# Other places for the background steps of the conv-GeGLU layers, in a two-network fp32 kernel

## The chip, the cores and the metric

One program on one core of a Trainium2 chip. The metric is the device time of one execution in microseconds, the median of several runs. The kernel before takes 2448.88 us (three runs: 2448.77, 2448.88, 2451.74).

Engines in the text: PE (TensorE, matrix products), DVE (VectorE), ACT (ScalarE), POOL (GpSimd) and SP (SyncE, which issues most DMAs). PSUM is the memory of eight banks into which PE writes.

## The reference

Two small networks run one behind the other on a sequence of 512 positions with 1024 channels, in fp32. The first has a pooling mixer, a conv-GeGLU layer (ffn0), windowed attention and a second conv-GeGLU layer (ffn1). The second has an S5 mixer, an MLP, an SSD mixer and an MLP; its norms are shifted and scaled by a vector `mod` worked out from a conditioning vector `c`.

```
def conv_glu_ffn(h, w_in, conv_w, conv_b, w_out):
    u = h @ w_in                                   # 1024 -> 2 * 2816
    up = jnp.pad(u, ((0, 0), (CONV_WIDTH - 1, 0), (0, 0)))
    u = sum(conv_w[k] * up[:, k:k + S] for k in range(CONV_WIDTH)) + conv_b
    gate, val = jnp.split(u, 2, axis=-1)
    return (jax.nn.gelu(gate, approximate=True) * val) @ w_out
...
x = x + rms_norm(conv_glu_ffn(rms_norm(x, ffn_pre_g), ...), ffn_post_g)
...
mod = silu(c) @ ada_w[i] + ada_b[i]                # 1024 -> 6144, for the second network
```

## The kernel before

Activations are held transposed: 128 channels on the partitions, 512 positions along the row. Each fp32 operand is split into a high and a low part, and each product is three matmuls (L220 to L222: hi·hi, lo·hi, hi·lo). A weight chunk comes by a DMA into `ws` (three buffers), ACT copies the high part `wh` (L205) and DVE subtracts for the low part `wl` (L206).

**A conv-GeGLU layer** (`ffn_layer`) has 22 column tiles of the hidden width, in three phases (8, 8 and 6 tiles). A phase handles its tiles two by two. For one pair PE fills four PSUM banks (`pp`: gate and value of two tiles); `scaled` (L969, DVE) multiplies each bank by the norm's factor into `u` and so frees it; `glu` does the convolution (ACT, then DVE L975 and L976), gelu on ACT, the product (L983) and the split into `hi` (ACT L319) and `lo` (DVE L321). The pool for these products has four banks, so the matmuls of one pair need those of the one before read. After phases 0 and 1 `project` multiplies by the part of `w_out` for the tiles so far, in eight output tiles, and `evac` copies (phase 0, ACT L1007) or adds (phase 1, DVE L1009) each into `f`. The last phase's products are done by the tail (`tail_`), first for the first 256 positions and then for the second 256, and the next layer's norm (`acc`, L305 sums over channels, L311 and L314 the factor) and its first projection are joined to it: the first half of the next layer's head needs only the first half of the tail. `seam` (L815) orders this.

**Background work** is done by generators that a layer steps on through `bg[0](n)`: each generator in the list is taken n steps further (class `Background`). In ffn0 it is `s5_tables` (tables for the S5 mixer, many 128x512 and 128x128 operations on DVE, L681 to L793; 72 steps), and what has not been done by the end of the layer's body is drained there (`end_tables`). In ffn1 it is `vecmat` (L477), which works out `mod` (12 blocks) and a like product with S5's input weights (2 blocks), 60 steps in all, and in addition Toeplitz matrices for S5. A block of `vecmat` takes eight tiles `as` of 128x512 (256 KB each, two buffers, DMA issued by POOL, L495). DVE multiplies the first by its factor (L498) and multiplies and adds the next seven into `aa` (L500); after every second tile the generator yields, so a step is two tiles. At a block's end ACT casts `aa` into bf16 three times (L512), DVE taking off each time what has been cast (L514), and PE sums over the partitions with twelve matmuls (L484, four for each part), which `mod` is built from. Since `aa` has one buffer, the next block's L498 follows the casts.

A layer's Python code gives only priorities: the scheduler of the framework orders each engine's instructions ahead of time, with the program's order as priority and a model of durations. Each engine then works through its instructions in that fixed order.

In the layer's body (L1013 to L1046) steps stand in three places: two at the beginning (L1015), `rate` behind each pair (L1039), and one behind each of the eight evacuations of a down phase (L1043). Phase 0 has three pairs in the body (the first belongs to the head), phase 1 four and the last three. `rate` is 5 in ffn0, 4 in ffn1.

Of the kernel before, what the change touches and what calls it, by code (L numbers as in the profile page):

```python
# [62 lines left out]
def net_kernel(ctx: ExitStack, tc: tile.TileContext, I: dict, out: bass.AP, parts=ALL):  # L63
# [27 lines left out]
    def psmm():  # L91
        return psm.tile([P, 512], F32, tag="mm", name=nm("mm"))
# [741 lines left out]
    bg = [no_bg]  # L834
# [125 lines left out]
    def ffn_layer(l, phases, late=None, rate=3):  # L960
# [52 lines left out]
        def body_():  # L1013
            hh, hl = S_["pre"].hi, S_["pre"].lo
            bg[0](2)  # L1015
            for ph, (j0, j1) in enumerate(phases):
                final = ph == len(phases) - 1
                if final and late is not None:
                    late()
                for j in range(j0 if ph else 2, j1, 2):  # L1020
                    pp = {(i, q): psmm() for i in range(2) for q in range(2)}
                    src = [chunks(win, 0, KD, i * F1 + j * P) for i in range(2)]
                    if final and j == j1 - 2:
                        chs = [list(c) for c in src]
                        for q in range(2):
                            for i in range(2):
                                for ch in chs[i]:
                                    mm_chunk(pp[i, q], ch, q, hh, hl, KD, FULL)
                        for i in range(len(tl.runs)):
                            tl.load_apart(i)  # L1030
                    else:
                        for _ in range(2):
                            for i in range(2):
                                ch = next(src[i])
                                for q in range(2):
                                    mm_chunk(pp[i, q], ch, q, hh, hl, KD, FULL)
                    for q in range(2):
                        glu(j + q, *(scaled(pp[i, q]) for i in range(2)))
                    bg[0](rate)  # L1039
                if not final:  # L1040
                    def evac(n, ps, span):
                        down(n, ps, span, ph == 0, False)
                        bg[0](1)  # L1043

                    project(wout, j0, j1 - j0, 0, (0, 8), S_["ah"], S_["al"], evac)
                    S_["ah"], S_["al"] = [], []  # L1046
# [914 lines left out]
    def end_tables():  # L1961
        work.drain()
        close("stk", "psb")
        bgps[0] = psmm
# [5 lines left out]
    for name in names:  # L1970
# [6 lines left out]
        if name == "ffn0":  # L1977
            layer = ffn_layer(0, ((0, 8), (8, 16), (16, 22)),
                              lambda: rope_c.update(rope_tables()) if "attn" in names else None, 5)
            seam(prev, layer)  # L1980
            close("plf")
            if tables_due and "pool" not in names:
                start_tables()
            layer.body()
            if tables_due:
                end_tables()
                tables_due = False
        elif name == "attn":
            layer = attention_layer(opened("atc"), opened("atps", space=PSUM), rope_c or rope_tables())
            seam(prev, layer)  # L1990
            layer.body()
            close("atc", "atps")
        elif name == "ffn1":
            layer = ffn_layer(1, ((0, 8), (8, 16), (16, 22)), rate=4)
            seam(prev, layer)
            if tables_due:
                start_tables()
                end_tables()
                tables_due = False
            if ada_due[:1] == [0]:  # L2000
                start_ada(ada_due.pop(0))
            if toeplitz_due:
                work.gens.append(s5_toeplitz(opened("stz"), dr))
                toeplitz_due = False
            layer.body()
            work.drain()
            close("stz", "adp")
        else:
            if tables_due:
                start_tables()  # L2010
                end_tables()
                tables_due = False
            if toeplitz_due:
                work.gens.append(s5_toeplitz(opened("stz"), dr))
                toeplitz_due = False
            if ada_due and (name[-1] == "1" or name == "ssd" or ada_due[0] == 0):
                start_ada(ada_due.pop(0))
                work.drain()
                close("stz", "adp")
            if name == "s5":  # L2020
                layer = s5_layer(dr, opened("s5p"), opened("s5ps", space=PSUM))
            elif name == "ssd":
                layer = ssd_layer(opened("sdp"), dpl, opened("sdps", space=PSUM))
            else:
                layer = mlp_layer(int(name[-1]))
            seam(prev, layer)
            if name == "mlp0" and ada_due:
                start_ada(ada_due.pop(0))
            layer.body()
            work.drain()  # L2030
            close("adp", "s5p", "s5ps", "sdp", "sdps")
# [41 lines left out]
```

## Time and profile before

| | |
|---|---|
| median of three runs | 2448.88 us |
| profiled execution | 2448.6 us |
| its span | 2446.9 us |
| mean PE clock granted | 0.974 of full |
| PE busy | 2303.6 us |
| DVE busy | 1707.1 us |
| ACT busy | 1139.7 us |
| ffn0's end (last up matmul to attention's first projection) | 417.4 to 481.20 |
| ffn1's end (the same, to S5's first projection) | 1036.6 to 1087.75 |

The profiled execution is 1.7 us longer than its span and 0.3 us shorter than the median. Times in the rows below are microseconds from the span's start. In brackets behind an instruction stands how long its engine had been idle, and what ended the wait.

### The profile page before, as it was taken

The page shows a single profiled execution, that of the slowest core. Times are in us where ns is not written, and L with a number is a line of the kernel's source. Part 1 is how long each engine was busy: PE and PEld are TensorE (multiplying, and loading weights), DVE is VectorE, ACT ScalarE, POOL GpSimd, SP SyncE. Part 2 cuts the span into 40 slices and gives each one's busy share as a digit, 9 for nine tenths or more (in the row PEclk, how much of TensorE's full clock was granted, in tenths as well). Part 3 has the DMA queues.
Part 4 walks back from the last instruction along what each step waited for, and adds up shares of the span by engine and source line. Part 5 has one row for each costly group of instructions (what it writes and reads, how often), then busy time and mean ns, then how long its engine had stood idle before and what let it go on. Part 6 is the DMA issues. An engine that isn't in the chain of part 4 may idle for free.

```text
span 2446.9 us, 33813 instructions
## 1 busy us (share of the span) xinstructions
PE 2303.6 (94%) x12477; PEld 1948.5 (80%) x12477; DVE 1707.1 (70%) x3064; ACT 1139.7 (47%) x2030; POOL 419.4 (17%) x596
## 2 busy tenths in 40 slices
PE   6989998788989999988799999999999999999998
PEld 6778877775878888787779878789878878888888
DVE  6896979767778697886646666666777788533333
ACT  6533535466675343455534333344555554422322
POOL 2001120002431211110301011010242340200110
PEclk9999999889989999989899999999999999999999
DMA  4224453311465655455742555542333332233322
GB/s 123 81 91 137 145 152 118 106 59 45 127 193 174 195 179 190 159 198 170 220 141 73 172 164 189 186 151 74 113 95 99 108 101 89 91 95 98 100 82 74
DMA packets 265190, 315.52 MB, mean 129 GB/s; under 512 B 34161, under 2 KB 222401, under 8 KB 264001
## 3 DMA queue, kind: packets, MB, share of 16 engines
q1 hardware_dynamic: 220929, 233.64, 30.5%
q0 software_dynamic: 19648, 62.41, 8.1%
q10 hardware_dynamic: 24448, 17.31, 2.2%
q8 instruction: 98, 1.61, 0.3%
q14 instruction: 67, 0.55, 0.1%
HBM read 289.12 MB, written 24.18 MB: 128 GB/s over the span
## 4 chain that ended last, share of the span: by engine, by line
PE 63%; DVE 14%; DMA 10%; issue 7%; ACT 4%; POOL 1%; SPq 0%; ACTq 0%; DVEq 0%; POOLq 0%
PE mm L221 18%; PE mm L220 18%; PE mm L222 18%; DMA as<-in_ada_w 6%; DVE wl L206 3%; DVE aa L500 1%; ACT wh L205 1%; PE pb L1746 1%; PE mm L1676 1%; PE mm L1677 1%; PE mm L1678 1%; DMA tz<-d_k 1%; DVE u L969 1%; PE py L1417 1%; DVE aa L514 1%
## 5 line engine op out<-in xcount | busy, mean ns | idle before, releaser
L220 PE MATMUL mm<-h,wh 128*128 128x512 f32 (+1 forms) x1792 | 665.6, 373 | 31.9 <-ACT h L429 16.2
L221 PE MATMUL mm<-h,wh 128*128 128x512 f32 (+1 forms) x1792 | 666.7, 373 | 7.4 <-DVE h L430 3.7
L222 PE MATMUL mm<-h,wl 128*128 128x512 f32 (+1 forms) x1792 | 663.4, 371 | 0.2 <-DVE wl L206 0.2
L205 ACT ACTIVATE wh<-ws 128x1024 fp32r<-128x1024 f32 (+1 forms) x367 | 387.1, 1059 | 505.6 <-PE mm L221 427.6
L206 DVE TENSOR_TENSOR wl<-ws,wh 128x1024 fp32r<-128x1024 f32 (+1 forms) x367 | 462.3, 1262 | 210.9 <-ACT wh L205 204.5
L220 PEld LDWEIGHTS mm<-h,wh 128*128 128x128 f32 x1792 | 346.2, 194 | 90.5 <-ACT h L429 17.4
L221 PEld LDWEIGHTS mm<-h,wh 128*128 128x128 f32 x1792 | 347.0, 194 | 64.9 <-DVE h L398 5.7
L222 PEld LDWEIGHTS mm<-h,wl 128*128 128x128 f32 x1792 | 346.9, 194 | 55.6 <-issue 1.8
L220 PE MATMUL mm<-hi,wh 128*128 128x512 f32 (+1 forms) x1056 | 371.5, 356 | 10.4 <-ACT wh L205 10.0
L221 PE MATMUL mm<-lo,wh 128*128 128x512 f32 (+1 forms) x1056 | 372.5, 354 | 3.4 <-DVE lo L321 3.0
L222 PE MATMUL mm<-hi,wl 128*128 128x512 f32 (+1 forms) x1056 | 372.1, 354 | 3.1 <-DVE wl L206 3.1
L220 PEld LDWEIGHTS mm<-hi,wh 128*128 128x128 f32 x1056 | 202.0, 192 | 38.4 <-ACT wh L205 11.4
L221 PEld LDWEIGHTS mm<-lo,wh 128*128 128x128 f32 x1056 | 202.2, 191 | 30.4 <-DVE lo L321 4.8
L222 PEld LDWEIGHTS mm<-hi,wl 128*128 128x128 f32 x1056 | 201.8, 191 | 30.1 <-DVE wl L206 4.0
L500 DVE SCALAR_TENSOR_TENSOR aa<-as,cond,aa 128x512 f32<-128x512 f32 x168 | 131.0, 780 | 112.0 <-DMA as<-in_ada_w 110.9
L1298 POOL TENSOR_TENSOR r<-r 128x512 f32<-128x512 f32 x64 | 87.7, 1374 | 670.7 <-ACT r L1294 484.3
L512 ACT ACTIVATE ab<-aa 128x512 bf16<-128x512 f32 x78 | 51.7, 662 | 118.1 <-DVE aa L500 81.1
L321 DVE TENSOR_TENSOR lo<-r,hi 128x512 fp32r<-128x512 f32 x64 | 47.2, 743 | 76.7 <-ACT hi L319 76.6
L495 POOL DMA_DIRECT2D as<-in_ada_w x96 | 51.6, 538 | 241.7 <-DVE aa L500 120.7
L1319 DVE SCALAR_TENSOR_TENSOR x<-mm,mod,x 128x512 f32<-128x512 f32 (+1 forms) x76 | 48.9, 662 | 58.4 <-PE mm L222 58.3
L319 ACT ACTIVATE hi<-r 128x512 fp32r<-128x512 f32 x64 | 40.4, 631 | 71.1 <-POOL r L1298 71.0
L297 DVE TENSOR_TENSOR acc<-acc,sq 128x256 f32<-128x256 f32 (+1 forms) x148 | 62.5, 440 | 9.3 <-ACT sq L296 5.2
(507 smaller groups left out, 3669.0 us busy)
## 6 DMA issues: line engine op xcount, KB each, us to landing
ws<-in_mlp_w SPq DMA_DIRECT2D x124, 512.0 KB, 4.0
ws<-in_ffn_w_in SPq DMA_DIRECT2D x88, 512.0 KB, 4.4
as<-in_ada_w POOLq DMA_DIRECT2D x96, 256.0 KB, 3.2
as<-in_ada_w SPq DMA_DIRECT2D x96, 256.0 KB, 3.4
ws<-in_m_w_in SPq DMA_DIRECT2D x41, 512.0 KB, 3.7
ws<-in_ffn_w_out SPq DMA_DIRECT2D x40, 512.0 KB, 3.4
ws<-in_w_o SPq DMA_DIRECT2D x16, 512.0 KB, 3.9
ct<-d_tab POOLq DMA_DIRECT2D x8, 1024.0 KB, 5.7
```

Of the source, the lines that this page charges most:

```text
L205: A.activation(h_, s_, AF.Copy)
L206: V.tensor_tensor(l_, s_, f(h_), ALU.subtract)
L220: T.matmul(ps, wh, xh, start=first, stop=False)
L221: T.matmul(ps, wh, xl, start=False, stop=False)
L222: return T.matmul(ps, wl, xh, start=False, stop=last).ins
L297: V.tensor_tensor(dst, dst, sq[:, a:b], ALU.add)
L321: return hi_, V.tensor_tensor(lo[:, ts], src, f(hi[:, ts]), ALU.subtract)
L495: queue.dma_start(st, W[k * P:(k + 1) * P, cb * 512:(cb + 1) * 512])
L500: V.scalar_tensor_tensor(acc, st, col(k), acc, ALU.mult, ALU.add)
L512: A.activation(pv[j], av, AF.Copy)
L1298: G.tensor_tensor(r, r, r, ALU.mult)
L1319: V.scalar_tensor_tensor(xT[n][:, ts], ps, md(i, 5, n), xT[n][:, ts], ALU.mult, ALU.add)
```

## The change

Three edits in the conv-GeGLU layers. In the last phase no background steps are taken behind the last pair. Behind each evacuation of the down phases two steps are taken and not one. In ffn1 `rate` is the default 3 and not 4 (ffn0 keeps its 5).

```diff
@@ body_ of ffn_layer
                     for q in range(2):
                         glu(j + q, *(scaled(pp[i, q]) for i in range(2)))
-                    bg[0](rate)
+                    if not (final and j == j1 - 2):
+                        bg[0](rate)
                 if not final:
                     def evac(n, ps, span):
                         down(n, ps, span, ph == 0, False)
-                        bg[0](1)
+                        bg[0](2)
@@ the loop over the layers
         elif name == "ffn1":
-            layer = ffn_layer(1, ((0, 8), (8, 16), (16, 22)), rate=4)
+            layer = ffn_layer(1, ((0, 8), (8, 16), (16, 22)))
```

The steps that a layer takes, by place (beginning, pairs of phase 0, evacuations, pairs of phase 1, evacuations, pairs of the last phase): ffn0 2+15+8+20+8+15 = 68 before and 2+15+16+20+16+10 = 79 after; ffn1 2+12+8+16+8+12 = 58 before and 2+9+16+12+16+6 = 61 after. What is left over is drained behind the body.

How the rows on the engines move, at three places. In the names a number is a buffer's.

First DVE, the last pair of ffn0 (`u`, `tg`, `tv` are the pair's; `wl` weights of the tail; `ph`, `cp`, `ct`, `cc`, `b` are of the tables). Before:

```order
L759 TENSOR_TENSOR cp_4073<-cp_4073,ct_4074 128x4x128
L975 SCALAR_TENSOR_TENSOR tg_4236<-u_4232,vec,tg_4236 128x511
L742 TENSOR_TENSOR b_825_4311<-bs_4029,s5k_1093 128x128
L975 SCALAR_TENSOR_TENSOR tv_4237<-u_4234,vec,tv_4237 128x511
L206 TENSOR_TENSOR wl_4222<-ws_4220,wh_4221 128x512
L729 TENSOR_SCALAR cc_4306<-pb_4303,s5sg 128x128
L730 TENSOR_SCALAR cc_4306<-pb_4303 128x128
L681 TENSOR_TENSOR ph_4268<-s5ph_1096,s5ph_1098 128x512
L682 TENSOR_TENSOR ph_4269<-s5ph_1097,s5ph_1099 128x512
L681 TENSOR_TENSOR ph_4274<-s5ph_1096,s5ph_1099 128x512
L682 TENSOR_TENSOR ph_4275<-s5ph_1097,s5ph_1098 128x512
L975 SCALAR_TENSOR_TENSOR tg_4254<-u_4250,vec,tg_4254 128x511
```

After, from the last pair's first `lo` (4389) to the tail's first evacuation (L1009):

```order
L321 TENSOR_TENSOR lo_4389<-tv_4379,hi_4388 128x512
L206 TENSOR_TENSOR wl_4488<-ws_4486,wh_4487 128x1024
L969 TENSOR_TENSOR u_4394<-mm_4229,rsx_805 128x512
L206 TENSOR_TENSOR wl_4539<-ws_4537,wh_4538 128x1024
L975 SCALAR_TENSOR_TENSOR tg_4396<-u_4392,vec,tg_4396 128x511
L975 SCALAR_TENSOR_TENSOR tv_4397<-u_4394,vec,tv_4397 128x511
L976 SCALAR_TENSOR_TENSOR tg_4396<-u_4392,vec,tg_4396 128x510
L206 TENSOR_TENSOR wl_4590<-ws_4588,wh_4589 128x1024
L976 SCALAR_TENSOR_TENSOR tv_4397<-u_4394,vec,tv_4397 128x510
L983 TENSOR_TENSOR tv_4397<-tv_4397,tg_4396 128x512
L321 TENSOR_TENSOR lo_4407<-tv_4397,hi_4406 128x512
L1009 TENSOR_TENSOR f_1948<-f_1948,mm_4442 128x256
```

The table rows no longer stand among the rows of the last pair; the pair's own rows and the tail's weights are what is left.

Then PE, from the tail of ffn0 to attention: L305 and L314 are the norm's sums for the first 256 positions (`pn_4639`), `mm_4846`, `mm_4756` and `mm_4801` products of the tail's second half, `mm_5057` and `mm_5058` attention's first projections. Before:

```order
L220 MATMUL mm_4846<-hi_4264,wh_4227 128x256
L221 MATMUL mm_4846<-lo_4265,wh_4227 128x256
L222 MATMUL mm_4846<-hi_4264,wl_4228 128x256
L305 MATMUL pn_4639<-ones,acc_4480 128x128 x2
L314 MATMUL pn_4639<-dg_4645,ones 128x128 x2
L220 MATMUL mm_5057<-h_4418,wh_5008 128x256
L220 MATMUL mm_5058<-h_4418,wh_5032 128x256
```

After:

```order
L222 MATMUL mm_4713<-hi_4406,wl_4352 128x256
L220 MATMUL mm_4756<-hi_3993,wh_4487 128x256
L221 MATMUL mm_4756<-lo_3994,wh_4487 128x256
L305 MATMUL pn_4639<-ones,acc_4480 128x128 x2
L222 MATMUL mm_4756<-hi_3993,wl_4488 128x256
L220 MATMUL mm_4756<-hi_4011,wh_4487 128x256
...
L220 MATMUL mm_4801<-hi_4011,wh_4538 128x256
L314 MATMUL pn_4639<-dg_4645,ones 128x128 x2
L221 MATMUL mm_4801<-lo_4012,wh_4538 128x256
```

The two sums stood between the tail's end and the next projection; now both stand inside the tail's second half.

Third ffn1, the first pair of phase 1, on DVE (`u_8520`, `u_8590` are the first `u` of that phase before and after; `aa_8391` and `aa_8325` the block of `vecmat` that is being summed there). Before:

```order
L206 TENSOR_TENSOR wl_8610<-ws_8608,wh_8609 128x1024
L514 TENSOR_TENSOR aa_8211<-aa_8211,ab_8382 128x512 x2
L498 TENSOR_SCALAR aa_8391<-as_8389,cond 128x512
L500 SCALAR_TENSOR_TENSOR aa_8391<-as_8393,cond,aa_8391 128x512
L206 TENSOR_TENSOR wl_8640<-ws_8638,wh_8639 128x1024
L969 TENSOR_TENSOR u_8520<-mm_8396,rsx_7033 128x512
L500 SCALAR_TENSOR_TENSOR aa_8391<-as_8572,cond,aa_8391 128x512
L500 SCALAR_TENSOR_TENSOR aa_8391<-as_8575,cond,aa_8391 128x512
L206 TENSOR_TENSOR wl_8670<-ws_8668,wh_8669 128x1024
L500 SCALAR_TENSOR_TENSOR aa_8391<-as_8578,cond,aa_8391 128x512
L969 TENSOR_TENSOR u_8522<-mm_8398,rsx_7033 128x512
```

After:

```order
L498 TENSOR_SCALAR aa_8325<-as_8323,cond 128x512
L487 TENSOR_REDUCE sums_8343<-pn_8330 128x4
L500 SCALAR_TENSOR_TENSOR aa_8325<-as_8327,cond,aa_8325 128x512
L531 TENSOR_TENSOR mod<-sums_8343,vec 128x4
L500 SCALAR_TENSOR_TENSOR aa_8325<-as_8346,cond,aa_8325 128x512
L500 SCALAR_TENSOR_TENSOR aa_8325<-as_8349,cond,aa_8325 128x512
L500 SCALAR_TENSOR_TENSOR aa_8325<-as_8416,cond,aa_8325 128x512
L500 SCALAR_TENSOR_TENSOR aa_8325<-as_8419,cond,aa_8325 128x512
L500 SCALAR_TENSOR_TENSOR aa_8325<-as_8422,cond,aa_8325 128x512
L500 SCALAR_TENSOR_TENSOR aa_8325<-as_8425,cond,aa_8325 128x512
L969 TENSOR_TENSOR u_8590<-mm_8466,rsx_7033 128x512
L969 TENSOR_TENSOR u_8592<-mm_8468,rsx_7033 128x512
```

Between the last `u` of phase 0 and the first of phase 1 DVE takes 24 tiles `as` before and 33 after. The first `u` stood behind two rows of its block and has now all eight in front of it. Between the last `u` of phase 1 and the first of phase 2 it is 23 before and 35 after.

On PE at the same place, behind the matmuls of that pair: `pn` are column sums, `ab` the cast `aa`, and `mm_8604` and `mm_8652` the next pair's first products. Before:

```order
L484 MATMUL pn_8556<-one_86,ab_8383 128x1
L484 LDWEIGHTS ab_8383
L484 MATMUL pn_8556<-one_86,ab_8383 128x1
L220 MATMUL mm_8604<-h_6596,wh_8609 128x512
L221 MATMUL mm_8604<-h_6597,wh_8609 128x512
L222 MATMUL mm_8604<-h_6596,wl_8610 128x512
```

After:

```order
L484 LDWEIGHTS ab_8317
L484 MATMUL pn_8330<-one_86,ab_8317 128x1
L484 LDWEIGHTS ab_8430
L484 MATMUL pn_8444<-one_86,ab_8430 128x1
L484 LDWEIGHTS ab_8430
L484 MATMUL pn_8444<-one_86,ab_8430 128x1
L484 LDWEIGHTS ab_8430
L484 MATMUL pn_8444<-one_86,ab_8430 128x1
L484 LDWEIGHTS ab_8430
L484 MATMUL pn_8444<-one_86,ab_8430 128x1
L220 MATMUL mm_8652<-h_6596,wh_8657 128x512
L221 MATMUL mm_8652<-h_6597,wh_8657 128x512
```

The next pair stood behind the sums of one block; now the first four sums of the following block (`ab_8430`, cast from `aa_8325`) stand before it as well.

## Rows read from the trace of the kernel before

**Rows 1.** The page, busy time of each engine; DMA issues, KB each, us to landing.

```profile
PE 2303.6 (94%) x12477; PEld 1948.5 (80%) x12477; DVE 1707.1 (70%) x3064; ACT 1139.7 (47%) x2030; POOL 419.4 (17%) x596
...
as<-in_ada_w POOLq DMA_DIRECT2D x96, 256.0 KB, 3.2
```

**Rows 2.** Timeline of PE, end of ffn0: start, us, instruction, idle before and releaser.

```profile
419.81 0.39 PE L220 MATMUL mm<-hi,wh 128*128 128x256 f32 x1 [2.43 <-ACT wh L205]
...
443.69 0.39 PE L221 MATMUL mm<-lo,wh 128*128 128x256 f32 x1 [1.78 <-DVE lo L321]
...
444.03 0.29 PE L220 MATMUL mm<-hi,wh 128*128 128x256 f32 x1
...
444.15 0.28 PE L221 MATMUL mm<-lo,wh 128*128 128x256 f32 x1
...
481.20 0.79 PE L220 MATMUL mm<-h,wh 128*128 128x256 f32 x2 [1.75 <-ACT h L429]
```

**Rows 3.** Windows there: length, engines' busy time, PE clock, DMA share, GB/s.

```profile
430.00:440.00 10.00, 7.51 (x36) 7.15 (x36) 10.00 (x17) 3.52 (x5) 1.14 (x2) 0.55 0.69 229
...
480.00:490.00 10.00, 8.25 (x48) 7.96 (x49) 10.00 (x29) 7.36 (x23) 0.00 (x0) 0.66 0.08 30
```

**Rows 4.** DVE by lines, 417 to 444: busy us, mean ns, idle before.

```profile
L759 DVE TENSOR_TENSOR cp<-cp,ct 128x512 f32<-128x512 f32 x3 | 2.0, 682 | 0.0
...
L757 DVE TENSOR_TENSOR cp<-cc,s5k 128x512 f32<-128x512 f32 x2 | 1.4, 683 | 0.0
...
L791 DVE SCALAR_TENSOR_TENSOR kt<-s5eye,s5dg,kt 128x16 f32<-128x16 f32 x3 | 0.7, 227 | 0.0
...
L742 DVE TENSOR_TENSOR b<-bs,s5k 128x128 f32<-128x128 f32 x1 | 0.3, 281 | 0.0
```

**Rows 5.** Timeline of PE, end of ffn1.

```profile
1041.03 0.58 PE L220 MATMUL mm<-hi,wh 128*128 128x256 f32 x1 [4.42 <-ACT wh L205]
...
1087.75 0.80 PE L220 MATMUL mm<-h,wh 128*128 128x256 f32 x2 [4.22 <-ACT h L429]
```

**Rows 6.** Windows, middle of ffn1.

```profile
735.00:1036.00 301.00, 300.06 (x1438) 244.34 (x1437) 246.74 (x365) 131.31 (x174) 55.08 (x103) 1.00 0.56 178
```

**Rows 7.** DVE by lines, 735 to 1037.

```profile
L500 DVE SCALAR_TENSOR_TENSOR aa<-as,cond,aa 128x512 f32<-128x512 f32 x84 | 62.8, 748 | 44.4 <-DMA as<-in_ada_w 44.0
```

**Rows 8.** Windows of DVE alone, ffn0's phase changes.

```profile
164.00:221.00 57.00, 41.11 (x72) 1.00 0.45 137
...
303.00:365.00 62.00, 49.69 (x88) 1.00 0.51 155
```

**Rows 9.** Timeline of DVE, ffn1: the last `u` of two phases, `as` chain.

```profile
790.70 0.68 DVE L969 TENSOR_TENSOR u<-mm,rsx 128x512 f32<-128x512 f32 x1
...
810.60 0.49 DVE L498 TENSOR_SCALAR aa<-as,cond 128x512 f32<-128x512 f32 x1 [0.70 <-ACT ab L512]
...
814.35 0.75 DVE L500 SCALAR_TENSOR_TENSOR aa<-as,cond,aa 128x512 f32<-128x512 f32 x1 [0.83 <-DMA as<-in_ada_w]
...
830.70 0.49 DVE L498 TENSOR_SCALAR aa<-as,cond 128x512 f32<-128x512 f32 x1 [0.70 <-ACT ab L512]
...
846.16 0.75 DVE L500 SCALAR_TENSOR_TENSOR aa<-as,cond,aa 128x512 f32<-128x512 f32 x1 [2.32 <-DMA as<-in_ada_w]
...
926.99 0.68 DVE L969 TENSOR_TENSOR u<-mm,rsx 128x512 f32<-128x512 f32 x1
...
970.45 0.48 DVE L498 TENSOR_SCALAR aa<-as,cond 128x512 f32<-128x512 f32 x1 [1.12 <-ACT wh L205]
...
991.83 0.49 DVE L498 TENSOR_SCALAR aa<-as,cond 128x512 f32<-128x512 f32 x1 [0.70 <-ACT ab L512]
```

**Rows 10.** Timeline of POOL, an issue of the chain.

```profile
811.38 0.54 POOL L495 DMA_DIRECT2D as<-in_ada_w  x1 [3.78 <-DVE aa L498]
```

**Rows 11.** Timeline of PE, column sums behind the first pairs of phases 1, 2.

```profile
857.02 0.45 PE L484 MATMUL pn<-one,ab 128*128 128x1 bf16 x12
...
991.22 0.35 PE L484 MATMUL pn<-one,ab 128*128 128x1 bf16 x8
```

## The prediction

> **What bounds the kernel now.** I read the page first. TensorE (PE) is busy for 94% of the span, and VectorE (DVE) for 70% [rows 1], so where PE waits is where the time can change. The background's transfers, 96 of `as` on POOL's queue at a median of 3.2 us, matter only where something of the layers stands behind them.
>
> Then I read the two ends of the conv-GeGLU layers in the chain of PE. At the end of ffn0 the last up matmul is over by 417.4 (the first row of [rows 2], 419.81 less its wait of 2.43), and attention's first projection begins at 481.20: 63.8 us. The work between is the tail, 288 matmuls of 256 columns, which follow each other every 0.12 us at full clock (444.03 to 444.15), so 34.6 us. The other 29 us are waits: for weight splits, for the last `lo` (443.69), and for the normalised rows of the next layer (481.20), and a clock that falls to its lower level of 1.2 GHz: 0.55 of full in 430 to 440 and 0.66 in 480 to 490 [rows 3]. In the same 430 to 440 DVE is busy for all of the 10 us.
>
> What DVE does there is in [rows 4]: of 417 to 444 the tables for S5 take 14.6 us (L759 2.0; seven lines of two or so 128x512 operations at 1.4, as L757 is; L791 0.7; eight operations on 128x128 at 0.28, as L742 is), and the rest is the layer's own. The background stands between the layer's instructions, and delays the `lo` that PE waits for.
>
> ffn1 has the same end, 1036.6 to 1087.75, 51.1 us [rows 5]. Its middle, 735 to 1036, is another matter: PE is busy for 300.06 of 301 us, and DVE 246.74 [rows 6]. In this stretch PE loses nothing, though DVE waits 44.0 us for `as` DMAs, 84 of them [rows 7].
>
> **The change part by part.** The instructions are the same in number on every engine; only their places change. Counted in the generators' steps, ffn0 takes 68 steps of the tables before, and drains the 4 that are left of 72 behind its last pair; now it would take 79, so the tables end in the first pair of the last phase.
>
> *The end of ffn0.* By the order DVE has no table work in the last pair and the tail. Taking 14.6 us away brings the last `lo` from 26 us after the last up matmul (443.69 less 417.4) to some 12 us after it, so that the tail, which begins with the chunks of earlier pairs, need not wait for it. PE's order also has the norm's two sums (L305, L314) between matmuls of the tail's second half, so attention can follow without a gap. 34.6 us of matmuls and 1 to 5 us of first wait (2.43 now) make 36 to 40, with a lost half clock 44: the gain against 63.8 is 20 to 28. The lower clock of 480 to 490 can go too: 0.66 of 10 us lost 3.4. I take −28, near the upper end of 20 to 28, since the clock and the wait are likely to go together; range −20 to −31.
>
> *The middle of ffn0.* Two steps behind each of 16 evacuations put about 15 us more of table work (counted in the order, with the durations of [rows 4]) between the last `u` of phase 0 and the first of phase 1, and 16 us between phases 1 and 2. DVE was busy for 41.11 of 57 us in the first stretch and 49.69 of 62 in the second [rows 8]: 15.9 and 12.3 us are free. The first fits, the second is 3.7 too much. +4, range 0 to +9.
>
> *The end of ffn1.* Before, 58 of the 60 steps were taken and two drained behind the last pair; now the 61 suffice before it. 51.1 becomes 36 to 42 by the same sum: −13, range −9 to −18.
>
> *The middle of ffn1.* This is the part that decides. A step fetches two `as` tiles of 256 KB through two buffers, and DVE adds each to `aa` (L500). Eight make a block, then ScalarE (ACT) casts it. The chain's pace in the trace: blocks begin (L498) at 810.60 and 830.70, 20.1 us apart, though DVE was free to take them, since the last L500 of a block still waited 2.32 us for its DMA; later 970.45 and 991.83, 21.4 us [rows 9]. The tile issued at 811.38 [rows 10] is used at 814.35: 2.97 us.
>
> By the order DVE before took 24 tiles between the last `u` of phase 0 (790.70) and the first `u` of phase 1; now it is 33, since 16 steps stand behind the 8 evacuations. Before, 24 tiles at 20.1 us per 8 are 60 us, in a stretch of 66 from 790.70 to PE's sums at the end of the first pair (857.02) [rows 11]: the chain had just room. Now 33 tiles stand ahead of four `u`. Four blocks have to be done: the block running ends some 9.8 us after 790.70, three more starts follow at p us each, the last block's seven L500 take 0.76p and the cast 1.3. With p = 19.7 the `u` can go at 876; they are wanted at 857. PE's next pair needs the four PSUM banks that they free, and PE's order puts that block's sums (four L484) ahead of it as well. DVE can't pass the L500s, so the wait is PE's: 19 us. In numbers, 3.76p − 55. The bounds: from 830.70 to the last L500 at 846.16 seven tiles take 15.5 us, 4.4 for a round of two, so with L500's own 0.75 a tile takes 3.7 on the mean; with 2.97 for each, four rounds a block, p is 17.3 and the wait 10. With p = 22 it is 28. I take 19.7, near the rows, since they are of this stretch.
>
> At phase 2 it is the same: before 23 tiles, now 35. The chain stands three tiles and a block's end short of a new block at 926.99, which begins near 939; three blocks and the rest later is 939 + 3.76p + 1.3, against 991.22 [rows 11]: 3.76p − 51, 23 at 19.7. Bounds 14 (p = 17.3) and 32 (22). Behind each stall PE begins at the lower clock, as in 480 to 490 [rows 3], 3.4 us each by that row: +6 for both, 0 to +7.
>
> The chain's pace is the term with the largest weight, so I weigh a rule against it. The row shows 2.97 us for a tile from issue to use, and the page's median from issue to landing is 3.2. The Trainium skill ("DMA: Bandwidth & Descriptors", Anatomy of one DMA) gives 2.0 us and bytes/436e3 for such a DMA, which is an estimate of 2.6 us for 256 KB, and in "Latency and other measured facts" says that a lighter load on HBM makes the fixed part smaller. By it a block in the stall, where the weights rest, would take about 16 us, the stalls would be 5 and 9, and the sum would come out at 2432, which is rival 1 below. The trace disagrees while weights flow (20.1 a block); no row shows the chain alone.
>
> *The sum*: −28 + 4 − 13 + 19 + 23 + 6 = +11. On the profiled execution's 2448.6 us (span 2446.9 and 1.7 around it) that is 2459.6; the median of the runs shown is 0.3 higher, so 2460. With the terms of the likely case at their bounds it stays within 2454 and 2478.
>
> **The rivals.**
> 1. *The chain speeds up where it is waited for.* Once PE stands, the weights' three buffers are full and `as` has the DMA engines to itself, so p falls below what the trace shows with weights beside it. For it: 2.97 us for a tile, and L500's waits that end by DMA, not by POOL. Against it: 20.1 and 21.4 us with DVE free. At p = 17.3 the stalls are 10 and 14: −28 + 4 − 13 + 30 = −7, 2442; with no stall at all −37, 2412. The two stalls and their clock (7.52p − 106 + 6) equal the 37 gained at p = 18.2, and the kernel is faster by over 5 us below 17.5. This is the one that ends faster. The rule of the Trainium skill above ("DMA: Bandwidth & Descriptors", Latency and other measured facts) speaks for it.
> 2. *Gains and stalls cancel*: p between 17.5 and 18.9, or a gain at the ends nearer its upper bounds: 2449, within 5 us either way. For it: both sums are near 40, with uncertain parts of 10 each; against it only that the nearest rows stand above 18.9.
> 3. *The change doesn't do what it says at the ends.* Without the tables the tail still waits for its weights, since PE's first waits there end with ACT's `wh` (2.43 and 4.42, [rows 2, 5]), behind DMA, and the gelus of the last pair. Then ffn0 gains 12 and ffn1 5, and the stalls remain: −12 + 4 − 5 + 48 = +35, 2484. Against it: DVE is full in 430 to 440, and the last `lo` is what PE waits for at 443.69.
>
> **How the numbers follow.** Forecast, 2454 to 2478: 0.46. Rival 1: 0.24. Rival 2: 0.18. Rival 3: 0.12. The range that leaves 2 in 10 out is 2432 to 2480: it takes in rival 2, and rival 1 from 2442 a third of the way to its case without stalls, but not that case, nor most of rival 3. 0.2% is 4.9 us, about what a measurement of this kernel can tell from no change. Faster by more: rival 1, 0.24; within: 0.18; slower: the forecast and rival 3, 0.58.
>
> **What would show it.** Right: in ffn0 the stretch from the last up matmul to attention's first projection is under 45 us, no tables among DVE's work there; in ffn1 two waits of PE, the first near 833 (857 less the 24 gained before it) and the second a phase later, that end with a `u` or with the cast L512, 15 to 25 us each, while L500 stands waiting for `as` behind them. Wrong, with its step: no PE wait over 5 us there (the pace, or the place of the L500s); a tail that still takes over 50 us with DVE idle in it (then weights or ACT set it); new waits of PE in ffn0's down phases over 10 us (the free time of DVE there is not where the tables stand).

## The result, and the profile after

The changed kernel takes 2476.03 us, median of four runs (2469.76 to 2477.88), the kernel before 2450.31 (four runs, 2448.77 to 2456.92). The ratio is 1.0095, with a 95% interval of 1.0068 to 1.0122: slower by about 1%, or 23 us. The profiled execution after is the fastest of its four, 2469.76 us with a span of 2468.0; against the span before, 2446.9, that is +21.1 us, and the stages below add up to it. The other three runs are 4 to 8 us longer, and no trace tells where.

| stage, us (profiled executions) | before | after | difference | forecast |
|---|---|---|---|---|
| start to the third pair's `u` of ffn0 (161.28, 161.53) | 161.3 | 161.5 | +0.2 | 0 |
| to the last up matmul of ffn0 (417.4, 421.9) | 256.1 | 260.4 | +4.3 | +4 |
| ffn0's end, to attention's first projection (481.20, 459.00) | 63.8 | 37.1 | −26.7 | −28 |
| attention, to ffn1's body (721.60, 694.79) | 240.4 | 235.8 | −4.6 | 0 |
| ffn1's body, to its last up matmul (1036.6, 1061.7) | 315.0 | 366.9 | +51.9 | +48 |
| ffn1's end, to S5's first projection (1087.75, 1106.04) | 51.1 | 44.3 | −6.8 | −13 |
| the rest | 1359.2 | 1362.0 | +2.8 | 0 |

**ffn0's end.** The timeline of PE after (start, length, instruction, idle before and what ended it), which answers to [rows 2]:

```profile
421.70 0.39 PE L222 MATMUL mm<-h,wl 128*128 128x512 f32 x1
421.93 0.28 PE L220 MATMUL mm<-hi,wh 128*128 128x256 f32 x1
...
445.40 0.61 PE L305 MATMUL pn<-ones,acc 128*128 128x128 f32 x4
...
450.40 0.60 PE L314 MATMUL pn<-dg,ones 128*128 128x128 f32 x4
...
459.00 0.28 PE L220 MATMUL mm<-h,wh 128*128 128x256 f32 x1
```

The tail follows the last up matmul (421.70) at once, the norm's two sums stand inside it (445.40 and 450.40), and attention's projection comes without a wait at 459.00. On DVE the last `lo` that the tail needs starts 8.5 us behind the last up matmul where it was 26. Before:

```profile
442.95 0.69 DVE L321 TENSOR_TENSOR lo<-tv,hi 128x512 fp32r<-128x512 f32 x1
```

After:

```profile
430.39 0.69 DVE L321 TENSOR_TENSOR lo<-tv,hi 128x512 fp32r<-128x512 f32 x1 [0.70 <-ACT hi L319]
```

In windows (length, busy time of PE, PEld, DVE, ACT and POOL, PE clock, DMA share, GB/s) this stretch and the two stalls of ffn1 are:

```profile
422.00:459.00 37.00, 36.12 (x298) 35.52 (x297) 26.35 (x60) 17.00 (x36) 0.00 (x0) 1.00 0.26 86
830.00:850.00 20.00, 2.04 (x15) 1.62 (x16) 9.92 (x16) 4.07 (x7) 4.29 (x8) 0.55 0.48 148
995.00:1016.00 21.00, 2.61 (x20) 2.08 (x21) 11.15 (x18) 4.75 (x7) 4.83 (x9) 0.52 0.42 140
```

In the first row PE is busy for 36.12 of 37 us at full clock, and DVE for 26.35 us; before, DVE was busy for all of 430 to 440 [rows 3], and for 46.69 us of the whole 63.8. In the other two PE does next to nothing, 2.04 of 20 and 2.61 of 21 us, and its clock is near the lower level (0.55 and 0.52). The transfers issued in the two stalls, with KB each and the median us from issue to landing, are in the first (830 to 850):

```profile
as<-in_ada_w POOLq DMA_DIRECT2D x8, 256.0 KB, 3.1
ws<-in_ffn_w_in SPq DMA_DIRECT2D x1, 512.0 KB
```

and in the second (995 to 1016):

```profile
as<-in_s_w_in POOLq DMA_DIRECT2D x9, 256.0 KB, 2.9
```

with one weight chunk of 512 KB beside them there too.

**ffn1's body.** All the waits of PE from 690 to 1130 that stand behind a column sum of the background, as one row (us in total, times, longest):

```profile
PE pn L484 <- ACT ab L512: 45.3, 14, 16.3
```

Before, that pair of lines had 2.4 us in 5 waits. The timeline of PE shows where they lie:

```profile
829.07 0.25 PE L484 MATMUL pn<-one,ab 128*128 128x1 bf16 x4 [0.66 <-ACT ab L512]
830.45 0.25 PE L484 MATMUL pn<-one,ab 128*128 128x1 bf16 x4 [1.14 <-ACT ab L512]
831.92 0.27 PE L484 MATMUL pn<-one,ab 128*128 128x1 bf16 x4 [1.21 <-ACT ab L512]
848.48 0.27 PE L484 MATMUL pn<-one,ab 128*128 128x1 bf16 x4 [16.29 <-ACT ab L512]
...
995.61 0.26 PE L484 MATMUL pn<-one,ab 128*128 128x1 bf16 x4 [4.80 <-ACT ab L512]
997.34 0.27 PE L484 MATMUL pn<-one,ab 128*128 128x1 bf16 x4 [1.48 <-ACT ab L512]
998.73 0.27 PE L484 MATMUL pn<-one,ab 128*128 128x1 bf16 x4 [1.12 <-ACT ab L512]
1014.18 0.26 PE L484 MATMUL pn<-one,ab 128*128 128x1 bf16 x4 [15.19 <-ACT ab L512]
```

The first place (829.07 to 848.48, 19.3 us of waits together) is the end of phase 1's first pair, the second (995.61 to 1014.18, 22.6 us) that of phase 2's: the places of [rows 11]. The other 3.4 us are six shorter waits of the same kind, five of them just ahead of the second place. And on DVE, for [rows 9]:

```profile
793.09 0.49 DVE L498 TENSOR_SCALAR aa<-as,cond 128x512 f32<-128x512 f32 x1 [0.70 <-ACT ab L512]
...
813.14 0.49 DVE L498 TENSOR_SCALAR aa<-as,cond 128x512 f32<-128x512 f32 x1 [0.70 <-ACT ab L512]
...
832.52 0.48 DVE L498 TENSOR_SCALAR aa<-as,cond 128x512 f32<-128x512 f32 x1
...
847.01 0.75 DVE L500 SCALAR_TENSOR_TENSOR aa<-as,cond,aa 128x512 f32<-128x512 f32 x1 [0.69 <-DMA as<-in_ada_w]
847.68 1.28 DVE L969 TENSOR_TENSOR u<-mm,rsx 128x512 f32<-128x512 f32 x2
...
936.54 0.48 DVE L498 TENSOR_SCALAR aa<-as,cond 128x512 f32<-128x512 f32 x1
...
958.10 0.49 DVE L498 TENSOR_SCALAR aa<-as,cond 128x512 f32<-128x512 f32 x1
...
979.54 0.49 DVE L498 TENSOR_SCALAR aa<-as,cond 128x512 f32<-128x512 f32 x1 [0.70 <-ACT ab L512]
...
998.71 0.49 DVE L498 TENSOR_SCALAR aa<-as,mod 128x512 f32<-128x512 f32 x1 [0.70 <-ACT ab L512]
...
1012.27 0.75 DVE L500 SCALAR_TENSOR_TENSOR aa<-as,mod,aa 128x512 f32<-128x512 f32 x1 [0.91 <-DMA as<-in_s_w_in]
1012.94 1.28 DVE L969 TENSOR_TENSOR u<-mm,rsx 128x512 f32<-128x512 f32 x2
```

A block begins (L498), seven tiles come in (the last L500 at 847.01), and only then DVE gets to the `u` (847.68) that PE's banks wait for. The blocks are 20.0 and 19.4 us apart at the first place and 21.6, 21.4 and 19.2 at the second, where 19.7 was taken. The trace puts PE's wait down to the cast for the column sums; by its row the first `u` is done 0.2 us earlier at the first place and 0.6 at the second. Both stand behind the same last L500, and no run tells which of the two would hold PE alone.

DVE's waits for tiles in the body were 44.4 us before [rows 7]. After, by lines:

```profile
L500 DVE SCALAR_TENSOR_TENSOR aa<-as,cond,aa 128x512 f32<-128x512 f32 x84 | 63.0, 750 | 60.8 <-DMA as<-in_ada_w 60.1 <-DVE aa L500 0.2
```

Not all of the 51.9 us is waiting. By lines PE has 168 column sums in the body after and 144 before, since the last two blocks were drained behind it: 10.7 us of PE against 7.0. And behind each stall its products run at the lower clock, 9 of them (848.61 to 852.46) and 12 (1014.31 to 1019.56) at 0.43 us where they take 0.23: 1.8 and 2.5 us.

**ffn1's end**, for [rows 5], on PE:

```profile
1066.59 0.58 PE L220 MATMUL mm<-hi,wh 128*128 128x256 f32 x1 [4.90 <-ACT wh L205]
...
1106.04 0.28 PE L220 MATMUL mm<-h,wh 128*128 128x256 f32 x1
```

The first wait is as long as before (4.90, it was 4.42); the second, for `h` at the end, is gone. PE waits for ACT's `wh`, and ACT for the weights:

```profile
1065.48 1.06 ACT L205 ACTIVATE wh<-ws 128x1024 fp32r<-128x1024 f32 x1 [2.21 <-DMA ws<-in_ffn_w_out]
```

**Why ffn0's middle lost 4.3 us.** PE's groups by lines that belong to the tables, in the 256 us before and the 260 after. Before:

```profile
L784 PE MATMUL pb<-ident,vp 128*128 128x128 f32 x48 | 7.2, 271 | 0.0
L786 PE MATMUL pb<-cp,b 128*32 128x128 f32 x96 | 5.1, 285 | 0.0
L725 PE MATMUL pb<-ident,cs 128*128 128x128 f32 x12 | 2.6, 300 | 0.0
```

After:

```profile
L784 PE MATMUL pb<-ident,vp 128*128 128x128 f32 x64 | 9.6, 272 | 0.0
L786 PE MATMUL pb<-cp,b 128*32 128x128 f32 x128 | 6.8, 285 | 0.0
L725 PE MATMUL pb<-ident,cs 128*128 128x128 f32 x14 | 3.1, 300 | 0.0
```

16 + 32 + 2 matmuls stood in ffn0's end and now stand in the middle, 4.6 us of PE's time (7.2 + 5.1 + 2.6 against 9.6 + 6.8 + 3.1). PE waits there no more than before (1.7 us, it was 1.4): it is its own work that has moved. The same 4.6 us are part of what ffn0's end gained.

### The profile page after: what moved, and what is told of

Read it like the earlier page. It is cut to its first block, busy times and chain, and to the rows that moved or that the text cites. A ratio compares the mean times of both kernels' runs of the same rounds, so it can differ in the third digit from the quotient of the medians.

```text
span 2468.0 us, 33837 instructions
## 1 busy us (share of the span) xinstructions
PE 2299.5 (93%) x12477; PEld 1940.9 (79%) x12477; DVE 1713.1 (69%) x3064; ACT 1143.0 (46%) x2030; POOL 420.3 (17%) x596
## 4 chain that ended last, share of the span: by engine, by line
PE 70%; DVE 12%; DMA 8%; ACT 4%; issue 4%; POOL 1%; SPq 0%; ACTq 0%; DVEq 0%; POOLq 0%
PE mm L221 21%; PE mm L220 21%; PE mm L222 20%; DMA as<-in_ada_w 6%; DVE wl L206 3%; DVE aa L500 1%; ACT wh L205 1%; PE pb L1747 1%; PE mm L1677 1%; PE mm L1678 1%; PE mm L1679 1%; DMA ws<-in_ffn_w_out 1%; DMA tz<-d_k 1%; PE py L1418 1%; ACT s L1208 0%
## 5 line engine op out<-in xcount | busy, mean ns | idle before, releaser
L500 DVE SCALAR_TENSOR_TENSOR aa<-as,cond,aa 128x512 f32<-128x512 f32 x168 | 130.3, 776 | 131.6 <-DMA as<-in_ada_w 130.2
```

What stands on the lines that cost most here:

```text
L500: V.scalar_tensor_tensor(acc, st, col(k), acc, ALU.mult, ALU.add)
```

## The experiments

The variants set three things in a conv-GeGLU layer: `rate`, `ev` (steps behind an evacuation: 1 before, 2 after) and `skip` (no steps behind the last pair: off before, on after). Of their code only what differs is shown. The three last columns are stages of each kernel's one profiled execution, in us; the time is the median of all its runs:

| kernel | time, median | ratio to before, 95% interval | ffn0's end | ffn1's body | ffn1's end |
|---|---|---|---|---|---|
| before | 2450.31 | | 63.8 | 315.0 | 51.1 |
| after | 2476.03 | 1.0068 to 1.0122 | 37.1 | 366.9 | 44.3 |
| e1, ffn0's part alone | 2427.24 | 0.9879 to 0.9912 | 37.1 | 314.1 | 50.9 |
| e2, ffn1's part alone | 2505.37 | 1.0193 to 1.0225 | 64.6 | 370.3 | 44.5 |
| e3, four `as` buffers | 2420.16 | 0.9846 to 0.9876 | 37.4 | 315.8 | 40.2 |
| e6, one load in eight | 2426.83 | 0.9875 to 0.9904 | 37.1 | 315.1 | 41.7 |
| e5, two `aa` buffers | 2448.72 | 0.9970 to 0.9989 | 37.1 | 342.5 | 42.2 |
| e7, ffn1 at rate 5, one step | 2455.43 | 1.0000 to 1.0020 | 37.1 | 341.3 | 47.8 |
| e11, ffn1 at rate 3, one step | 2462.80 | 1.0025 to 1.0049 | 37.2 | 312.7 | 86.1 |
| e8, e1 with four `as` buffers | 2419.72 | 0.9841 to 0.9871 | 37.1 | 312.4 | 39.2 |
| b0, the same again | 2421.21 | 0.9855 to 0.9881 | 37.2 | 312.4 | 41.5 |
| b1, fewer steps in ffn0's phase 1 | 2430.29 | 0.9892 to 0.9918 | 49.0 | 312.5 | 40.2 |
| b2, before with four `as` buffers | 2438.31 | 0.9927 to 0.9951 | 63.9 | 310.9 | 41.4 |
| e10, e7 with four `as` buffers | 2426.03 | 0.9876 to 0.9910 | 37.1 | 317.9 | 41.0 |

**One part alone (e1, e2).** In the layer's call:

```diff
 e1 (ffn0 as changed):
-            layer = ffn_layer(1, ((0, 8), (8, 16), (16, 22)))
+            layer = ffn_layer(1, ((0, 8), (8, 16), (16, 22)), rate=4, ev=1, skip=False)
 e2 (ffn1 as changed):
-                              lambda: ... if "attn" in names else None, 5)
+                              lambda: ... if "attn" in names else None, 5, ev=1, skip=False)
```

> The change in ffn0 alone (two steps behind each evacuation, none behind the last pair); ffn1 as before the change (rate 4, one step behind each evacuation, steps behind the last pair). Theory (the gain is at ffn0's end, the loss is the as chain in ffn1's down phases): +4.6 at ffn0's middle, -26.8 at its end and -4.7 behind it, as the profile after shows, so -27 against before: 2423 us, 2417 to 2430; no wait of PE over 2 us between phases in ffn1. Rival (the loss comes from ffn0's part too, through work that it pushes into attention or later): 2440 or more.

> The change in ffn1 alone; ffn0 as before. Theory: the stalls of 18.5 and 28.1 us, 5.4 us of slower clock behind them, -6.8 at ffn1's end and +2.8 behind it: +48, 2498 us, 2488 to 2508. Rival (the stalls come about only since ffn1 starts in another state after the changed ffn0): below 2470.

2427.24 and 2505.37 us, both within their ranges. The two parts add up: −26 and +52 are +26, about what the whole change cost (23 to 26). In e1 PE's waits between ffn1's phases are 1.8 us in all, in e2 they are 48.8 us behind column sums. The gain is ffn0's, the loss ffn1's, and neither needs the other. How much of ffn0's gain comes from DVE's time and how much from the new order on PE was not tried. Attention took 236.8 us in e1 and 238.8 in e2 (there ffn0 is unchanged), against 240.4 and 235.8 before and after: the −4.6 of the first table is not the change's for sure.

The edit that leaves out the steps behind the last pair should have no effect of its own. With the other two in place the generators have ended before that pair (79 of 72 and 61 of 60 steps), so a step there would find nothing to do. This is read from the code; no run left that edit out.

**No transfers to wait for (e6).** Of a block's eight loads in ffn1 only the first is kept, and DVE multiplies that tile eight times, so `mod` and what follows from it are other numbers. The condition keeps the loads that SP issues, outside ffn1.

```diff
-                st = pool.tile([P, 512], F32, tag="as", bufs=2, name=nm("as"))
-                queue.dma_start(st, W[k * P:(k + 1) * P, cb * 512:(cb + 1) * 512])
+                if k == 0 or queue is nc.sync:
+                    st = pool.tile([P, 512], F32, tag="as", bufs=2, name=nm("as"))
+                    queue.dma_start(st, W[k * P:(k + 1) * P, cb * 512:(cb + 1) * 512])
```

> The changed kernel, but in ffn1's background seven of a block's eight loads are left out: DVE multiplies the block's first tile eight times. DVE's, ACT's and PE's work stays. Theory (PE waits for DVE, and DVE for as DMAs): a block costs 0.5 + 7 x 0.75 and a boundary of 4.6, some 10 us, under what the phases have room for; PE waits under 3 us at the two places, 2425 to 2435 us. Rival (it is the amount of DVE work in front of the u, not the transfers): PE still waits 10 us or more at each, 2450 or more.

2426.83 us, within the range. The same 84 multiplications of DVE take the same 62.9 us, without waiting (by lines; the code is one line longer, so L500 is L501):

```profile
L501 DVE SCALAR_TENSOR_TENSOR aa<-as,cond,aa 128x512 f32<-128x512 f32 x84 | 62.9, 748 | 1.2
```

PE has no wait at all in the body, though by the trace 33 and 32 tiles still stand between the phases. DVE's work in front of the `u` is not what held PE; the waits for transfers were.

**Four buffers (e3).** `bufs=4` for `as`; `tz` goes from two to one to make room.

```diff
-                st = pool.tile([P, 512], F32, tag="as", bufs=2, name=nm("as"))
+                st = pool.tile([P, 512], F32, tag="as", bufs=4, name=nm("as"))
-            tz = pool.tile([P, 8, P], F32, tag="tz", bufs=2, name=nm("tz"))
+            tz = pool.tile([P, 8, P], F32, tag="tz", bufs=1, name=nm("tz"))
```

> The changed kernel with four buffers for the background's tiles as instead of two (and one instead of two for the Toeplitz tiles tz, which pays for the room). Theory (the chain's pace is a DMA's latency shared by two buffers): a tile every 1.2 us or so instead of 2.1, a block in 13 us or less, the stalls at 3.76p - 55 and 3.76p - 51 are gone: 2476 - 47 + 3 = 2432 us, 2422 to 2442. Rival A (the transfers' throughput beside the weights sets the pace): blocks still take 19 to 20 us, over 2465. Rival B (the boundary between blocks, cast and subtract, sets it): 2450 to 2465.

2420.16 us, a little under the range. A block takes 12.7 us (timeline of DVE), and the waits for tiles in the body are 6.8 us where they were 44.4 before the change and 60.8 after it:

```profile
807.10 0.48 DVE L498 TENSOR_SCALAR aa<-as,cond 128x512 f32<-128x512 f32 x1 [0.70 <-ACT ab L512]
...
819.78 0.49 DVE L498 TENSOR_SCALAR aa<-as,cond 128x512 f32<-128x512 f32 x1 [0.70 <-ACT ab L512]
```

```profile
L500 DVE SCALAR_TENSOR_TENSOR aa<-as,cond,aa 128x512 f32<-128x512 f32 x84 | 62.8, 748 | 6.8 <-DMA as<-in_ada_w 5.7
```

The transfers can come faster by far; two buffers held them back. The order is not what helps: 33 tiles stand at each of the two places. Nor is it the single `tz`, since e6 has no stall with two of them. The steps of the changed kernel are harmless once a block is shorter than the room for it.

**The boundary between blocks (e5).** `bufs=2` for `aa`, `as` again at two.

```diff
-                    acc = pool.tile([P, 512], F32, tag="aa", bufs=1, name=nm("aa"))
+                    acc = pool.tile([P, 512], F32, tag="aa", bufs=2, name=nm("aa"))
```

> The changed kernel with two buffers for the sum aa instead of one (and one instead of two for tz, which pays for the room). Now the next block's first multiply need not wait for the casts. Theory (a block is seven tiles at a DMA's pace, 14.6 us, and a boundary of 4.6, in which no load runs): the boundary falls to one load's wait, p from 19.5 to some 17, the stalls from 18 and 28 to 9 and 18: 2456 us, 2448 to 2464. Rival (the loads are behind by themselves and the boundary lies in their shadow): the stalls stay, over 2468.

2448.72 us, at the lower end of the range; ffn1's body is 342.5 us instead of 366.9. Blocks are 18.6 and 17.8 us apart at the first place:

```profile
791.74 0.49 DVE L498 TENSOR_SCALAR aa<-as,cond 128x512 f32<-128x512 f32 x1 [0.36 <-DMA as<-in_ada_w]
...
810.35 0.49 DVE L498 TENSOR_SCALAR aa<-as,cond 128x512 f32<-128x512 f32 x1 [1.37 <-DMA as<-in_ada_w]
...
828.11 0.48 DVE L498 TENSOR_SCALAR aa<-as,cond 128x512 f32<-128x512 f32 x1
```

Against 20.0 and 19.4 in the changed kernel that is 1.5 us less on the mean. At the second place it is 19.1, 19.2 and 19.7 (from 942.37) against 21.6, 21.4 and 19.2, 1.4 less. By the sum's rule (3.76 times the pace at each of two places) that would be worth 11 of the 24.4 us that the body is shorter. But the order on DVE has changed too: by the trace 28 and 30 tiles stand between the phases here, not 33 and 35, and five tiles at this pace (19 us for eight) are 12 us at each place. So e5 does not tell what the boundary alone is worth. The transfers are enough to explain the loss, since e3 removes it all with the boundary left as it was.

**Other numbers of steps (e7, e11).**

```diff
 e7:  +            layer = ffn_layer(1, ((0, 8), (8, 16), (16, 22)), rate=5, ev=1)
 e11: +            layer = ffn_layer(1, ((0, 8), (8, 16), (16, 22)), rate=3, ev=1)
```

> The change in ffn0; in ffn1 one step behind each evacuation, five behind each pair, none behind the last: 63 of 60 steps, so that nothing is drained, and by the order 24 tiles between phases 0 and 1 and 24 between phases 1 and 2. Theory (the number of tiles between the phases decides; 24 have room): no stall over 4 us in the middle, and the end of ffn1 at 44 or less instead of 51: 2421 us, 2416 to 2429. Rival (five steps behind a pair, ten tiles in 24.5 us, outrun the chain): each pair of ffn1 loses some 2 us, 2435 or more.

2455.43 us, 26 above the range: this missed, and the rival's time was right (2435 or more), though its loss of 2 us a pair was too small. The 24 tiles between the phases do fit (0.83 us of wait is the longest there), but in phase 1 each pair behind the first now has one whole block in front of its four `u`, on DVE, and the phase takes 113.5 us (815.65 to 929.15) instead of 89.1:

```profile
857.88 0.48 DVE L498 TENSOR_SCALAR aa<-as,cond 128x512 f32<-128x512 f32 x1
...
874.77 0.75 DVE L500 SCALAR_TENSOR_TENSOR aa<-as,cond,aa 128x512 f32<-128x512 f32 x1 [1.76 <-DMA as<-in_ada_w]
...
883.66 0.48 DVE L498 TENSOR_SCALAR aa<-as,cond 128x512 f32<-128x512 f32 x1
...
909.12 0.48 DVE L498 TENSOR_SCALAR aa<-as,cond 128x512 f32<-128x512 f32 x1
```

and on PE one of the waits:

```profile
876.24 0.27 PE L484 MATMUL pn<-one,ab 128*128 128x1 bf16 x4 [12.60 <-ACT ab L512]
```

Blocks begin 25.8 and 25.5 us apart, though the last L500 stands only some 17 us behind the block's beginning (874.77): behind it DVE first has the four `u` and the convolution of the pair to do, and the casts, before the next block. That is longer than PE needs for a pair, 22.3 us (phase 1's four pairs took 89.1 us before, not the 24.5 each that I had written). The number of tiles was not enough to count; where in the pair a block ends counts too.

> The changed kernel with ffn1's evacuations at one step (rate 3 stays): 45 of 60 steps, 15 are drained behind the last pair. By the order 23 tiles between phases 0 and 1, 23 between 1 and 2, and 24 left at the last u. Theory (the second step behind an evacuation makes the stalls, not the rate): no stall in the middle; three blocks of 19.5 us remain for the end, whose sums the next layer's norm waits for: 51 becomes 65 to 75, so 2441 us, 2432 to 2455. Rival (rate 3 takes part in the stalls): a wait of PE over 5 us between the phases.

2462.80 us, above the range. The body has no stall (312.7 us, its longest wait of PE 0.5), so the second step behind an evacuation makes the stalls, and rate 3 by itself does not. The three blocks that were left for the end cost more than I took, 86.1 us instead of 65 to 75, since the norm's sums stand behind the last block's in PE's order:

```profile
1066.78 0.27 PE L484 MATMUL pn<-one,ab 128*128 128x1 bf16 x4 [12.28 <-ACT ab L512]
...
1086.41 0.26 PE L484 MATMUL pn<-one,ab 128*128 128x1 bf16 x4 [15.09 <-ACT ab L512]
...
1093.06 1.23 PE L305 MATMUL pn<-ones,acc 128*128 128x128 f32 x4 [0.26 <-DVE sums L487]
...
1098.28 0.80 PE L220 MATMUL mm<-h,wh 128*128 128x256 f32 x2 [1.84 <-ACT h L429]
```

**Which version is fastest (e8, b0, b1, b2, e10).** All have four `as` buffers and one `tz`, as e3.

```diff
 e8, b0: ffn0 as changed, ffn1 (rate=4, ev=1, skip=False)
 b1:     as b0, and in ffn0 ev=2 in phase 0, ev=1 in phase 1, rate 6 in the last phase
 b2:     ffn0 (rate 5, ev=1, skip=False), ffn1 (rate=4, ev=1, skip=False)
 e10:    ffn0 as changed, ffn1 (rate=5, ev=1)
```

> The change in ffn0, ffn1's steps as before the change, with four buffers for as (and one for tz). Against the run with ffn0's part alone it shows what the buffers do where nothing stalls: only the drain behind the last pair can get shorter. Theory: the middle the same within 2 us, the end of ffn1 between 40 (four buffers and the change) and 51: 2423 us, 2418 to 2428. Rival (the four buffers gain elsewhere than at the stalls, for example less waiting of DVE in the pairs): under 2415.

> The change in ffn0, ffn1's steps as before the change, four buffers for as (and one for tz), once more and with more rounds, for comparison with the next two: 2420 us, 2417 to 2424.

> As the run before it, but in ffn0 two steps behind the evacuations of phase 0 only, one behind those of phase 1, and six behind each pair of the last phase, so that the tables still end before its last pair (73 of 72 steps). Theory (DVE's free time of 12.3 us between phases 1 and 2 holds one step behind each evacuation, not two): of the 4.3 us lost in ffn0's middle about 2 come back, the end stays at 37: 2418 us, 2414 to 2421. Rival (the loss comes from phase 0's part alone, or DVE in the last phase's pairs delays the tail instead): the same or 1 to 3 us more.

> The kernel before the change with four buffers for as (and one for tz) alone. Theory (the buffers only shorten what the drain leaves behind ffn1's last pair): ffn1's end 39 instead of 51, 2441 us, 2437 to 2445; ffn0's end as before. Rival (the gain of the run with the change in ffn0 and four buffers needs both): the same as before within 3 us.

> The change in ffn0, four buffers for as (one for tz), and in ffn1 one step behind each evacuation and five behind each pair, none behind the last: the steps that with two buffers cost 25 us in phase 1's pairs. Theory (those pairs lost their time since a block took longer than a pair; with four buffers it takes some 13 us): no loss in the middle, ffn1's end near 40: 2420 us, 2416 to 2424. Rival (the five steps cost DVE time in the pairs, whatever the buffers): 2430 or more.

e8 and b0 (2419.72 and 2421.21) and e3 (2420.16) are one time within their intervals: with four buffers ffn1's old and new steps are worth the same. b2 shows that the buffers gain 14 us by themselves, 10 of them at ffn1's end. The other 17 of b0's 31 us fall to ffn0's part, which gained 26 alone (e1): the two gains do not quite add up, and no stage shows where the 9 us between them are. Stages that no edit touches differ by as much as 5 us from profile to profile (the first one took 161.3 to 166.2). e8, b0 and b2 lie within their ranges.

b1 was a miss, 9 us over b0 and beyond its rival too. Its middle is 258.5 us, 1.9 less than the changed kernel's, which looks like the forecast; but only since 24 of the 50 matmuls of the tables now stand behind the last up matmul. The end takes 49.0 us, as the steps in the last phase make the tail wait for `wh` again:

```profile
436.90 0.58 PE L220 MATMUL mm<-hi,wh 128*128 128x256 f32 x1 [5.96 <-ACT wh L205]
```

ACT is late there because of the tables: it issues five of their stores (L793, `kt`) from 428.65 on, and by its row is free only at 433.8.

e10 lies 5 us over b0, in ffn1's body (317.9 against 312.4), not within its range. It is not the pairs of phase 1, which take 89.2 us against 88.7. e10 does all column sums in the body, 168 against b0's 144, 10.6 us of PE against 6.5, and has one wait of 1.6 us, in phase 0. The fastest kernels found are e3, e8 and b0: the change in ffn0 and four `as` buffers, for b0 0.9868 of before (0.9855 to 0.9881), 1.3% faster than before where the change as made is 1% slower.

## Why the prediction was right, and where it was not

- *The forecast.* Slower, by +11; measured +21 in the profile and +23 to +26 by medians (2476.03 against 2450.31 here, 2448.88 in the runs that the prediction had). Inside the range, and 16 us from the number. Of the 10 us in the profile 6.2 are ffn1's end, 3.9 its body, 1.8 the stages of ffn0 and the start, and −1.8 the remainder. That the median lies within the range is in part luck: it is 2 us from the upper end, and the range is narrower than the sum's own terms allow, whose bounds add up to −25 and +47, 2424 to 2496.
- *ffn0's end*, −28: −26.7. Each of its steps is in the trace: no table rows, the last `lo` early, the sums inside the tail, no gap before attention. But the 29 us that the prediction read as waits and clock held 4.6 us of the tables' matmuls on PE, and these were not saved but moved.
- *ffn1's body*, 19 + 23 + 6: PE's waits are 19.3 and 22.6 us at the two places, and the clock is at its lower level behind them, which costs 4.3 us and not 6. At the first place the pace was 19.7, as taken. At the second it was 20.7 on the mean, which makes 27 by 3.76p − 51; the shorter waits ahead of it, 3.2 us, belong to that number, and 25.8 is what the trace shows. The sum had left out the 3.7 us of column sums that move into the body. +51.9 against +48. e1, e2, e3 and e6 show that it is the transfers through two buffers, and that the second step behind an evacuation brings it on (e11).
- *Rival 1*, and the rule behind it: that a tile comes sooner once the weights rest. In the stall seven tiles took 14.5 us (832.52 to 847.01) and 13.6 (998.71 to 1012.27), against 15.5 before with weights beside them [rows 9], and a transfer landed 3.1 and 2.9 us after its issue, against 3.2 [rows 1]. That is a little sooner. With a boundary of 4.6 us, as before the change (846.16 to 850.74), it would make 18.2 to 19.1 us a block, an estimate. The prediction's estimate of about 16 us a block came from the fit of the Trainium skill ("DMA: Bandwidth & Descriptors", Anatomy of one DMA). The trace does not agree with it: the fit gives 2.6 us for 256 KB, and 3.1 and 2.9 were measured. Besides, only the last block of each place, and at the second the end of the one before, falls into the stall: PE stops at 828.4 and 990.8.
- *ffn1's end*, −13: −6.8. This is the term that was mis-sized. It carried ffn0's case over, but the first weights of the tail come late there too (4.90 us, ACT waiting for its DMA), and PE begins at the lower clock. Rival 3 had named that wait. With four buffers the tail begins without a wait in e3 and e8 (in e3 waits of 1.8 and 1.0 us for `wh` follow) and the end takes 39 to 41 us, near the 38 that the prediction had. In e6, with two buffers but one load in eight, the first wait is 0.25 us and the end 41.7, so the background's loads take part in making the weights late; how was not tried by itself.
- *ffn0's middle*, +4: +4.3, by another cause. The step that failed is "the second is 3.7 too much" for DVE. DVE held the steps (busy for 53.95 of 57 and 60.03 of 62 us in the windows of [rows 8], and PE waits no more than before); the 4 us are the tables' 50 matmuls on PE, which the sum had left out, although they belong to the steps that move. b1, built on the wrong cause, only moved 24 of them on, and lost 9 us in all.
- *The remainder*: 4.6 less in attention and 2.8 more behind ffn1 were not forecast, and the runs do not settle either: attention took 235.8 to 242.3 us in kernels that don't differ there.

## What to carry to other kernels

Background work that waits for transfers must not stand in an in-order queue ahead of what frees the main engine's buffers unless its own pace fits the room: count the transfers between two such places, and multiply by the pace that the trace shows for their number of buffers. The same steps are free or cost 50 us, by two more buffers. Work that is moved from one stage to another takes all its engines along: what PE does for it counts too.

## What the runs showed of the hardware

With two buffers a 256 KB tile came every 1.9 to 2.1 us in a stall in which little else was moved (one weight chunk beside 8 and 9 tiles, 148 and 140 GB/s at a DMA share of 0.48 and 0.42). A round of two took some 4.1 us there: the L500 that frees a buffer begins at 841.49, the next load is issued at 842.53, and its tile is used at 845.57. With four buffers the block of eight went from 19.4 to 12.7 us with weights beside it, so the transfers had room for that. I had not expected that the weights' traffic makes so little difference to the chain: 15.5 us for seven tiles beside it, 13.6 to 14.5 almost without.
